# A forward substitution spread over 128 partitions, and two scratch buffers exchanged, in a gated DeltaNet layer

## The chip, the cores and the metric

The kernel runs on one core of a Trainium2 chip. The metric is the device time of one execution in microseconds (us). A core has five engines that each take their own instructions in order: TensorE (PE) for matmuls, VectorE (DVE), ScalarE (ACT), GpSimd (POOL) and SyncE (SP), which here only issues DMA transfers. PE's weight loads are listed apart, as PEld. An engine waits for another by semaphores.

## The reference

One decoder layer over 1024 positions and a model width of 2048, in float32. A combined projection gives q, k, v of eight DeltaNet heads (group A), and u, v, z of eight channel groups with spatial gating (group B). Their outputs are joined and projected by `w_out`. In group A a triangular system is solved for each head and each chunk of 64 positions:

```python
L = jnp.where(strict, jnp.einsum('bhnid,bhnjd->bhnij', kb, k) * decay, 0.0)
rhs = jnp.concatenate([vb, kb * jnp.exp(gc)[..., None]], axis=-1)
sol = lax.linalg.triangular_solve(L + jnp.eye(C, dtype=L.dtype), rhs,
                                  left_side=True, lower=True, unit_diagonal=True)
...
mix = jnp.concatenate([o_a, o_b], axis=-1) @ w_out[l].astype(x.dtype)
h = h + mix
return rms_norm(h, final_norm_w)
```

## The kernel before

**Stages.** The sequence is worked off in two halves of 512 positions. In each half the projection goes tile by tile of 128 columns: first group A (tiles 0 to 31, in four head pairs), then group B (the blocks `vb` of w_vb, then tiles 32 to 47). After both halves comes the output projection (L1002), which takes seven products of sums of quarters of `w_out` and of the mixed outputs in place of eight products.

**Weights.** A tile has four chunks. SP loads a chunk (`wr`, 256 KB, three buffers), ACT rounds it to `wh` (L136), DVE takes the rest `wl` (L137), and PE does 12 matmuls with them (L238, L239, L241): `wh` with `xh`, `wh` with `xl`, `wl` with `xh`, four times. The loop `run` prepares up to four chunks ahead of the one that PE works on. Names carry tile and chunk: `wl_25_1` is the second chunk of tile 25, `acc_24` the sum of tile 24.

**Side tasks.** What follows a tile (convolution, swaps through DRAM, gates, the DeltaNet steps) is written as generators. `tick` counts down and resumes them between matmuls, so that the numbers which they yield set where their instructions stand among those of the projection. The compiler's scheduler then fixes one order for each engine. `task_z` (tiles 24 to 31) scales the finished tile into `pcz` on DVE (L404) and writes its SiLU `z` on ACT (L544).

**The substitution.** `task_pair` runs once for each head pair and half, eight times. The inverses of the diagonal blocks of 32 x 32 are wanted, 32 of them in a pair: the lower triangles come from DRAM (`ld`) into `fs`, one block on each of 32 partitions; 31 steps of a multiply (L566) and a subtract (L568) turn the identity, in the other half of `fs`, into the inverse; it goes to DRAM (`xd`) and comes back (`tn`, L574) with the positions on the partitions, where it is transposed into `tt` and used in matmuls. `W_DMA1` and `W_DMA2` are the ticks that are left for the transfers.

**Behind it.** The chunk outputs `at` (L649) are added to `o` (L650), normalised (L655 to L661), transposed through DRAM (four `swapo`, L430, then `ut`, L433, both issued by POOL), and multiplied by the gate `z` (L672). `at` and the `sp` of group B's spatial gating share the PSUM banks of `gen_bank`; `s` (L746) reads `sp` and frees one.

**Sums of w_out.** `w_sums` makes, in the first half and in the second, eight steps each: four quarters are loaded (`ws`, L831), combined on DVE (L833 to L837) and stored to DRAM (`wc_d`, L840) for the output projection. It starts `W_SUM0` ticks after it is spawned, and then goes on as its buffers come free.

Of the kernel before, what the change touches and what calls it, by code (L numbers as in the profile page):

```python
# [8 lines left out]
F32 = mybir.dt.float32  # L9
# [3 lines left out]
ALU = mybir.AluOpType  # L13
# [4 lines left out]
P = 128  # L18
DM = 2048
SEQ = 1024  # L20
T = 512
NHALF = SEQ // T
KT = DM // P
NT = T // P
# [7 lines left out]
def kernel(ctx, tc, x_tok, x_t, w_in, w_v0, w_vb, w_out, conv_w, norm_w, a_log, dt_bias,  # L32
                       hn_w, sgu_w, sgu_b, wsp_t, b_sp, fn_w, out):
    nc = tc.nc
# [4 lines left out]
    big = pool("big", bufs=4)  # L39
    wk = pool("wk", bufs=2)  # L40
    sm = pool("sm", bufs=2)
    dr = pool("dr", bufs=2, space=DRAM)
# [8 lines left out]
    def bc(ap, shape):  # L51
        return ap.broadcast_to(shape)
# [21 lines left out]
    for c in range(2):  # L74
        r = slice(c * 64, (c + 1) * 64)
# [378 lines left out]
    W_DMA2 = 18  # L454
# [36 lines left out]
    def task_q(hf, h, st, pr, acc):  # L491
# [32 lines left out]
        if hh == 1:  # L524
            spawn(task_pair(hf, h // 2, st, pr))
# [23 lines left out]
    def task_pair(hf, p, st, pr):  # L549
        gt, heads = st["gt"], pr["hd"]  # L550

        ld, xd = pr["ld"], pr["xd"]
        fs = big.tile([32, 2, 32, 32], F32, tag="b8", name=f"fs{hf}_{p}")
        lu, xu = fs[:, 0], fs[:, 1]
        ldv = ld.rearrange("h t (c s j) (z i) -> s z (h t c) j i", c=2, s=2, z=2)
        for s in range(2):
            nc.gpsimd.dma_start(lu[s * 16:(s + 1) * 16], ldv[s, s])
        nc.gpsimd.memset(xu, 0.0)
        nc.gpsimd.memset(xu.rearrange("u i j -> u (i j)")[:, ::33], 1.0)
        tmp = wk.tile([32, 256], F32, tag="fst", bufs=1, name=f"fst{hf}_{p}")  # L560
        yield W_DMA1

        for k in range(31):
            n, m = 31 - k, k + 1
            tv = tmp[:, 0:n * m].rearrange("u (i j) -> u i j", j=m)
            nc.vector.tensor_tensor(tv, bc(lu[:, k, k + 1:].unsqueeze(2), [32, n, m]),  # L566
                                    bc(xu[:, k:k + 1, 0:m], [32, n, m]), op=ALU.mult)
            nc.vector.tensor_tensor(xu[:, k + 1:, 0:m], xu[:, k + 1:, 0:m], tv, op=ALU.subtract)  # L568
            yield 1
        xdv = xd.rearrange("h t (c s j) i -> s (h t c) (j i)", c=2, s=2)  # L570
        for s in range(2):
            nc.sync.dma_start(xdv[s], xu[s * 16:(s + 1) * 16].rearrange("u i j -> u (i j)"))
        tn = wk.tile([P, 2 * NT, 32], F32, tag="tn", bufs=1, name=f"tn{hf}_{p}")
        nc.sync.dma_start(tn, xd.rearrange("h t p i -> p (h t) i"))  # L574
        yield W_DMA2

        for q in range(0, P, 32):
            nc.vector.transpose(tt[q:q + 32, :, q:q + 32], tn[q:q + 32])
# [2 lines left out]
        for c in range(2):  # L581
            a, b = c * 64, c * 64 + 32
# [3 lines left out]
        for c in range(2):  # L586
            b = c * 64 + 32
            nc.scalar.activation(ys[b:b + 32], yp[b:b + 32], AF.Copy, scale=-1.0)
        yield 3
        for c in range(2):  # L590
            a, b = c * 64, c * 64 + 32
# [3 lines left out]
        for c in range(2):  # L595
            a, b = c * 64, c * 64 + 32
# [48 lines left out]
        for h2, hd in enumerate(heads):  # L645
            nm, o = f"{hf}_{p}_{h2}", hd["o"]
# [28 lines left out]
    def new_pair(hf, p):  # L675
        return dict(kq=big.tile([P, 2, 2, T], F32, tag="b8", name=f"kq{hf}_{p}"),
                    ld=dr.tile([2, NT, P, 64], F32, tag="ld", name=f"ld{hf}_{p}"),
                    xd=dr.tile([2, NT, P, 32], F32, tag="xd", name=f"xd{hf}_{p}"),
                    hd=[{}, {}])

    def group_a(hf, xs, st):
# [86 lines left out]
    def group_b(hf, xs, st):  # L768

        env, sb = {}, {}  # L770
        spawn(w_sums([(hf, k) for k in range(HK)]))
        for blk in range(1, 4):
            for k2 in range(KT // 2):
# [46 lines left out]
    def w_quarter(b, cb, k):  # L820

        return w_out[b[1] * 2 + cb, b[0] * HK + k]

    def w_sums(ck):

        yield W_SUM0
        for cb, k in ck:
            q = {}
            for i, b in enumerate(((1, 1), (0, 1), (0, 0), (1, 0))):
                q[b] = wk.tile([P, 1, T], F32, tag=("cv", "bv")[i // 2], bufs=(3, 2)[i // 2], name=f"ws{cb}_{k}_{i}")  # L830
                nc.sync.dma_start(q[b], w_quarter(b, cb, k))  # L831
            yield 5
            nc.vector.tensor_tensor(q[1, 1], q[1, 1], q[0, 1], op=ALU.subtract)  # L833
            nc.vector.tensor_tensor(q[0, 1], q[0, 1], q[0, 0], op=ALU.subtract)
            yield 1
            nc.vector.tensor_tensor(q[0, 0], q[0, 0], q[1, 1], op=ALU.add)
            nc.vector.tensor_tensor(q[1, 0], q[1, 0], q[0, 0], op=ALU.subtract)  # L837
            yield 1
            for i, b in enumerate(((0, 1), (0, 0), (1, 1), (1, 0))):
                nc.sync.dma_start(wc_d[i, cb, k], q[b].rearrange("p o c -> p (o c)"))  # L840
            yield 3
# [238 lines left out]
```

## Time and profile before

| what | value |
|---|---|
| median of 3 runs | 1778.87 us (1775.11 to 1783.17) |
| the profiled execution | 1779.21 us, span 1777.5 us |
| mean granted clock of PE | 0.992 |
| PE busy | 1728.8 us, 97% |
| DVE busy | 1251.7 us, 70% |
| ACT busy | 738.5 us, 42% |
| POOL busy | 263.6 us, 15% |
| moved by DMA | 277.99 MB, mean 156 GB/s |

The span runs from the first to the last instruction; the execution's own time is 1.7 us longer. An engine's busy time says little of what sets the end: what PE waits for has to be read from its waits, and where a clock below 1.0 stands in a window, its matmuls take longer.

### The profile page before, as it was taken

The numbers are of one execution on the slowest core, as the hardware profiler recorded it, in microseconds if no ns is written. First come the engines' busy times: TensorE is split into PE (matmuls) and PEld (weight loads), VectorE is DVE, ScalarE is ACT, GpSimd is POOL, SyncE is SP. The second block draws the span as 40 slices with busy tenths as digits, with TensorE's granted clock in tenths as the row PEclk, the third lists the DMA queues.
The fourth block names the chain that finished last, engine by engine and source line by source line (L and its number), as shares of the span: only waits on it lengthen the run. The fifth ranks groups of instructions, "written<-read, shape, count | busy, mean of one in ns | idle before, by whom it ended". The sixth has DMA issues, their size and how long they took to land.

```text
span 1777.5 us, 27441 instructions
## 1 busy us (share of the span) xinstructions
PE 1728.8 (97%) x9334; PEld 1456.6 (82%) x9334; DVE 1251.7 (70%) x2945; ACT 738.5 (42%) x1678; POOL 263.6 (15%) x314
## 2 busy tenths in 40 slices
PE   9999999999999999998999999999989999999997
PEld 8778788888997788886878878889878888888885
DVE  7798797987747633757979789793863344767765
ACT  7543544445333222646344444532422234433454
POOL 4110131211201200203012112120020000200211
PEclk9999999999999999999999999999999999999998
DMA  7455445364458734426453645444884466766455
GB/s 239 128 134 145 108 124 144 91 169 133 132 172 260 258 108 126 130 69 153 126 134 92 164 106 149 134 116 117 248 277 133 118 188 199 223 191 193 144 190 190
DMA packets 190046, 277.99 MB, mean 156 GB/s; under 512 B 38064, under 2 KB 70864, under 8 KB 189648
## 3 DMA queue, kind: packets, MB, share of 16 engines
q1 hardware_dynamic: 185216, 263.60, 50.9%
q0 software_dynamic: 4544, 12.62, 3.0%
q8 instruction: 73, 1.20, 0.3%
q14 instruction: 69, 0.57, 0.1%
q10 hardware_dynamic: 144, 0.01, 0.0%
HBM read 220.54 MB, written 55.61 MB: 155 GB/s over the span
## 4 chain that ended last, share of the span: by engine, by line
PE 54%; DVE 9%; DMA 7%; ACT 2%; issue 2%; SPq 0%; POOL 0%; DVEq 0%; ACTq 0%; POOLq 0%
PE oa L1002 12%; PE acc L238 10%; PE acc L241 10%; PE acc L239 10%; PE vb L788 7%; DMA ws<-w_out 1%; DVE wl L137 1%; DVE cv L413 1%; DMA xres<-x_tok 1%; DMA wc_d<-ws 1%; DVE c L914 1%; PE p L621 1%; PE sp L744 1%; DMA wr<-w_in 1%; PE at L649 1%
## 5 line engine op out<-in xcount | busy, mean ns | idle before, releaser
L238 PE MATMUL acc<-xh,wh 128*128 128x512 f32 x1472 | 591.8, 402 | 1.0 <-ACT wh L136 1.0
L241 PE MATMUL acc<-xh,wl 128*128 128x512 f32 x1472 | 576.9, 392 | 7.5 <-DVE wl L137 7.5
L239 PE MATMUL acc<-xl,wh 128*128 128x512 f32 x1472 | 575.8, 391 | 0.0
L136 ACT CAST wh<-wr 128x512 fp32r<-128x512 f32 x368 | 225.7, 618 | 427.7 <-PE acc L239 270.6
L137 DVE TENSOR_TENSOR wl<-wr,wh 128x512 fp32r<-128x512 f32 x368 | 258.2, 704 | 154.2 <-ACT wh L136 151.2
L241 PEld LDWEIGHTS acc<-xh,wl 128*128 128x128 f32 x1472 | 277.1, 188 | 67.0 <-DVE wl L137 9.0
L238 PEld LDWEIGHTS acc<-xh,wh 128*128 128x128 f32 x1472 | 278.0, 189 | 57.7 <-issue 3.0
L239 PEld LDWEIGHTS acc<-xl,wh 128*128 128x128 f32 x1472 | 278.0, 189 | 51.5 <-issue 0.2
L1002 PE MATMUL oa<-who,a 128*128 128x512 f32 x864 | 267.9, 390 | 0.2 <-ACT who L136 0.2
L1002 PEld LDWEIGHTS oa<-who,a 128*128 128x128 f32 x864 | 162.6, 188 | 34.7 <-ACT who L136 0.6
L1002 PE MATMUL oa<-wlo,a 128*128 128x512 f32 x432 | 168.7, 390 | 0.6 <-DVE wlo L137 0.5
L137 DVE TENSOR_TENSOR wlo<-wro,who 128x512 fp32r<-128x512 f32 x108 | 79.4, 738 | 52.7 <-ACT who L136 52.2
L413 DVE SCALAR_TENSOR_TENSOR cv<-pc,cw,cv 128x511 f32<-128x511 f32 (+1 forms) x144 | 109.1, 758 | 9.6 <-ACT cv L410 8.2
L788 PE MATMUL vb<-whvb,xh 128*128 128x256 f32 x384 | 110.5, 288 | 0.0
L788 PE MATMUL vb<-wlvb,xh 128*128 128x256 f32 x384 | 108.6, 283 | 0.0
L788 PE MATMUL vb<-whvb,xl 128*128 128x256 f32 x384 | 108.6, 283 | 0.0
L136 ACT CAST who<-wro 128x512 fp32r<-128x512 f32 x108 | 66.6, 618 | 96.6 <-PE oa L1002 63.7
L1002 PEld LDWEIGHTS oa<-wlo,a 128*128 128x128 f32 x432 | 81.3, 188 | 18.5 <-DVE wlo L137 1.7
L566 DVE TENSOR_TENSOR fst<-fs 32x31 f32<-32x31 f32 (+15 forms) x248 | 89.3, 360 | 4.3
L568 DVE TENSOR_TENSOR fs<-fs,fst 32x31 f32<-32x31 f32 (+15 forms) x248 | 89.0, 359 | 4.1
L625 ACT ACTIVATE o<-p,g_egs 64x128 f32<-64x128 f32 x128 | 46.5, 363 | 84.3 <-DVE vz L624 81.6
L952 POOL TENSOR_TENSOR c<-c,fw 128x512 f32<-128x512 f32 x24 | 37.6, 1596 | 254.6 <-ACT sqh L950 254.6
(245 smaller groups left out, 2379.2 us busy)
## 6 DMA issues: line engine op xcount, KB each, us to landing
wr<-w_in SPq DMA_DIRECT2D x368, 256.0 KB, 3.3
ws<-w_out SPq DMA_DIRECT2D x64, 256.0 KB, 4.0
wc_d<-ws SPq DMA_DIRECT2D x64, 256.0 KB, 3.6
wro<-wc_d SPq DMA_DIRECT2D x64, 256.0 KB, 2.8
ar<-mix_d SPq DMA_DIRECT2D x56, 256.0 KB, 3.5
wrvb<-w_vb SPq DMA_DIRECT2D x48, 256.0 KB, 2.7
wro<-w_out SPq DMA_DIRECT2D x48, 256.0 KB, 2.8
xr<-x_t SPq DMA_DIRECT2D x32, 256.0 KB, 4.2
```

Of the source, the lines that this page charges most:

```text
L136: nc.scalar.copy(hi, src)
L137: nc.vector.tensor_tensor(lo, src, hi.bitcast(F32), op=ALU.subtract)
L238: nc.tensor.matmul(acc, hi[:, kk, :], xh, start=(k == 0), stop=False)
L239: nc.tensor.matmul(acc, hi[:, kk, :], xl, start=False, stop=(last and lo is None))
L241: nc.tensor.matmul(acc, lo[:, kk, :], xh, start=False, stop=last)
L413: nc.vector.scalar_tensor_tensor(cv[:, s:], acc[:, :T - s], w, cv[:, s:], op0=ALU.mult, op1=ALU.add)
L566: nc.vector.tensor_tensor(tv, bc(lu[:, k, k + 1:].unsqueeze(2), [32, n, m]), bc(xu[:, k:k + 1, 0:m], [32, n, m]), op=ALU.mult)
L568: nc.vector.tensor_tensor(xu[:, k + 1:, 0:m], xu[:, k + 1:, 0:m], tv, op=ALU.subtract)
L625: nc.scalar.activation(hd["o"][ra, t, :], pp[rq, :], AF.Copy, scale=gt["egs"][rq, h, t:t + 1])
L788: nc.tensor.matmul(a, l[:, tsl], r[:, k % 2, :], start=fl, stop=sp_, skip_group_check=True)
L952: nc.gpsimd.tensor_tensor(c, c, env["fw"][q], op=ALU.mult)
L1002: nc.tensor.matmul(acc[t], l[:, tsl], r[:, 0, :], start=fl, stop=sp_, skip_group_check=True)
```

## The change

The 32 systems of a pair are spread over 128 partitions: partition g*32 + u holds system u and those columns j of the inverse for which j mod 4 = g, eight of them. Step k then touches only the first k//4 + 1 of the eight columns, where before it touched k + 1. `fs` is loaded four times over, so eight loads take the place of two, four issued by POOL and four by SP; POOL's memsets are smaller, and one is made for each quarter of the partitions. The result goes out in one transfer instead of two. It comes back in pieces of 8 elements (32 bytes) into a new tile `tg`, where before a piece was 32 elements (128 bytes), and ACT copies `tg` into `tn` in natural order. `w_sums` takes its quarters from the buffers of `o` (2) and `gae` (3) instead of those of `cv` (3) and `bv` (2).

```diff
@@ task_pair
-        fs = big.tile([32, 2, 32, 32], F32, tag="b8", name=f"fs{hf}_{p}")
-        lu, xu = fs[:, 0], fs[:, 1]
+        fs = big.tile([P, 2, 32, 32], F32, tag="b8", name=f"fs{hf}_{p}")
+        lu, xu = fs[:, 0], fs[:, 1, 0:8].rearrange("u a (b m) -> u (a b) m", m=8)
         ldv = ld.rearrange("h t (c s j) (z i) -> s z (h t c) j i", c=2, s=2, z=2)
-        for s in range(2):
-            nc.gpsimd.dma_start(lu[s * 16:(s + 1) * 16], ldv[s, s])
-        nc.gpsimd.memset(xu, 0.0)
-        nc.gpsimd.memset(xu.rearrange("u i j -> u (i j)")[:, ::33], 1.0)
-        tmp = wk.tile([32, 256], F32, tag="fst", bufs=1, name=f"fst{hf}_{p}")
+        xf = xu.rearrange("u i m -> u (i m)")
+        nc.gpsimd.memset(xf, 0.0)
+        for g in range(4):
+            for s in range(2):
+                (nc.gpsimd, nc.sync)[g % 2].dma_start(lu[g * 32 + s:(g + 1) * 32:2], ldv[s, s])
+            nc.gpsimd.memset(xf[g * 32:(g + 1) * 32, 8 * g:8 * g + 33 * 7 + 1:33], 1.0)
+        tmp = wk.tile([P, 80], F32, tag="fst", bufs=1, name=f"fst{hf}_{p}")
         yield W_DMA1
 
         for k in range(31):
-            n, m = 31 - k, k + 1
+            n, m = 31 - k, k // 4 + 1
             tv = tmp[:, 0:n * m].rearrange("u (i j) -> u i j", j=m)
-            nc.vector.tensor_tensor(tv, bc(lu[:, k, k + 1:].unsqueeze(2), [32, n, m]),
-                                    bc(xu[:, k:k + 1, 0:m], [32, n, m]), op=ALU.mult)
+            nc.vector.tensor_tensor(tv, bc(lu[:, k, k + 1:].unsqueeze(2), [P, n, m]),
+                                    bc(xu[:, k:k + 1, 0:m], [P, n, m]), op=ALU.mult)
             nc.vector.tensor_tensor(xu[:, k + 1:, 0:m], xu[:, k + 1:, 0:m], tv, op=ALU.subtract)
             yield 1
-        xdv = xd.rearrange("h t (c s j) i -> s (h t c) (j i)", c=2, s=2)
-        for s in range(2):
-            nc.sync.dma_start(xdv[s], xu[s * 16:(s + 1) * 16].rearrange("u i j -> u (i j)"))
+        nc.sync.dma_start(xd, xf)
+        tg = wk.tile([P, 4, 2 * NT, 8], F32, tag="tg", bufs=1, name=f"tg{hf}_{p}")
+        nc.sync.dma_start(tg, xd.rearrange("(g u c s) (r m) -> (c s r) (g u) m", g=4, s=2, c=2, m=8))
+        yield W_DMA2 - 2
         tn = wk.tile([P, 2 * NT, 32], F32, tag="tn", bufs=1, name=f"tn{hf}_{p}")
-        nc.sync.dma_start(tn, xd.rearrange("h t p i -> p (h t) i"))
-        yield W_DMA2
+        nc.scalar.copy(tn.rearrange("p u (m g) -> p g u m", g=4), tg)
+        yield 2
@@ w_sums
-                q[b] = wk.tile([P, 1, T], F32, tag=("cv", "bv")[i // 2], bufs=(3, 2)[i // 2], name=f"ws{cb}_{k}_{i}")
+                q[b] = wk.tile([P, 1, T], F32, tag=("o", "gae")[i // 2], bufs=(2, 3)[i // 2], name=f"ws{cb}_{k}_{i}")
```

From here on the changed kernel's lines are four higher (L746 is L750), and inside `task_pair` up to three (L566 is L569, L568 L571).

**Tile 24 to 25, first pair.** On ACT before, at the change from tile 24 to 25 in the first pair of the first half (`cv_17` belongs to tile 17):

```order
L136 CAST wh_24_3_1295<-wr_24_3_1293 128x512
L410 ACTIVATE cv_17_1286<-pc_17_1284,cw 128x512
L136 CAST wh_25_0_1320<-wr_25_0_1318 128x512
L530 ACTIVATE cv_17_1286<-cv_17_1286 128x512
L136 CAST wh_25_1_1352<-wr_25_1_1350 128x512
L136 CAST wh_25_2_1374<-wr_25_2_1372 128x512
L136 CAST wh_25_3_1400<-wr_25_3_1398 128x512
L544 ACTIVATE z_0_1394<-pcz_0_1392 128x512
```

And at the same place with the change:

```order
L136 CAST wh_24_3_1304<-wr_24_3_1302 128x512
L410 ACTIVATE cv_17_1295<-pc_17_1293,cw 128x512
L530 ACTIVATE cv_17_1295<-cv_17_1295 128x512
L544 ACTIVATE z_0_1403<-pcz_0_1401 128x512
L136 CAST wh_25_0_1329<-wr_25_0_1327 128x512
L136 CAST wh_25_1_1361<-wr_25_1_1359 128x512
```

`z_0`, which needs all of tile 24, has moved from behind the four casts of tile 25 to ahead of them. DVE there with the change (the rows left out are 12 more of the substitution):

```order
L425 STREAM_TRANSPOSE pc_17_1293<-cv_17_1295 128x4x4x32
L404 TENSOR_TENSOR pcz_0_1401<-acc_24_1308,rb_715 128x512
L569 TENSOR_TENSOR fst_0_1243<-fs_0_1229 128x31
...
L571 TENSOR_TENSOR fs_0_1229<-fs_0_1229,fst_0_1243 128x25x2
L569 TENSOR_TENSOR fst_0_1243<-fs_0_1229 128x48
L137 TENSOR_TENSOR wl_25_0_1330<-wr_25_0_1327,wh_25_0_1329 128x512
L571 TENSOR_TENSOR fs_0_1229<-fs_0_1229,fst_0_1243 128x24x2
```

`pcz_0` and 15 instructions of the substitution now stand ahead of `wl_25_0`, and 19 more follow before `wl_25_1`; before, `wl_25_0`, the transpose and `wl_25_1` stood ahead of the first step of the substitution, and `pcz_0` behind its 15th. The second half has the same order.

**Ahead of `s_0`, half 1.** On DVE before, the last part of the chain from `at_3_0` to `s_0` (`ws_5_i` are the quarters of the sixth step of the sums):

```order
L137 TENSOR_TENSOR wl_41_1_6312<-wr_41_1_6309,wh_41_1_6311 128x512
L833 TENSOR_TENSOR ws_5_0_6996<-ws_5_0_6996,ws_5_1_6998 128x512
L834 TENSOR_TENSOR ws_5_1_6998<-ws_5_1_6998,ws_5_2_7000 128x512
L836 TENSOR_TENSOR ws_5_2_7000<-ws_5_2_7000,ws_5_0_6996 128x512
L137 TENSOR_TENSOR wl_41_2_6330<-wr_41_2_6327,wh_41_2_6329 128x512
L672 SCALAR_TENSOR_TENSOR o_3_0_5711<-ut_3_0_5703,hnw,z_6_4785 128x512
L837 TENSOR_TENSOR ws_5_3_7002<-ws_5_3_7002,ws_5_2_7000 128x512
L746 SCALAR_TENSOR_TENSOR s_0_6156<-sp_0_6151,lnw,brow 128x512
```

And with the change:

```order
L137 TENSOR_TENSOR wl_41_1_6352<-wr_41_1_6349,wh_41_1_6351 128x512
L676 SCALAR_TENSOR_TENSOR o_3_0_5751<-ut_3_0_5743,hnw,z_6_4824 128x512
L137 TENSOR_TENSOR wl_41_2_6370<-wr_41_2_6367,wh_41_2_6369 128x512
L750 SCALAR_TENSOR_TENSOR s_0_6196<-sp_0_6191,lnw,brow 128x512
```

The sums have left this stretch, and `o` stands ahead of `wl_41_2`.

**Sums among the weight loads.** On SP with the change, a piece of the stage between `wr_35_0` and `wr_38_2`:

```order
L187 DMA wr_36_0_6781<-w_in 128x512
L844 DMA wc_d<-ws_2_1_6693 128x512
L844 DMA wc_d<-ws_2_2_6695 128x512
L844 DMA wc_d<-ws_2_0_6691 128x512
L844 DMA wc_d<-ws_2_3_6697 128x512
L835 DMA ws_3_0_6799<-w_out 128x512
L835 DMA ws_3_2_6803<-w_out 128x512
L835 DMA ws_3_1_6801<-w_out 128x512
L835 DMA ws_3_3_6805<-w_out 128x512
L187 DMA wr_36_1_6807<-w_in 128x512
```

Eight transfers of the sums stand between two chunks of a tile. Before, the loads and stores of the sums were spread from tile 31 through the `vb` blocks up to `wr_42_3`, and in this place stood `wr_35_1` to `wr_45_0` with only loads of x and stores of the mixed outputs between them.

## Rows read from the trace of the kernel before

**Rows 1.** The page's busy table: busy us, share of span, instructions.

```profile
PE 1728.8 (97%) x9334; PEld 1456.6 (82%) x9334; DVE 1251.7 (70%) x2945; ACT 738.5 (42%) x1678; POOL 263.6 (15%) x314
```

**Rows 2.** Waits of PE: total us, times, longest us.

```profile
PE at L649 <- DVE s L746: 10.7, 2, 5.6
...
PE ds L632 <- DVE vz L624: 4.0, 10, 0.9
...
PE wp L611 <- DVE wq L612: 2.8, 3, 1.1
```

**Rows 3.** Windows behind the two long waits: us, busy of engines, PEclk, DMA share, GB/s.

```profile
580.00:584.00 4.00, 3.93 (x14) 3.52 (x15) 2.81 (x5) 0.91 (x5) 1.66 (x1) 0.53 0.77 232
1305.00:1311.00 6.00, 5.42 (x22) 4.97 (x22) 4.42 (x8) 2.43 (x10) 1.96 (x2) 0.52 0.84 281
```

**Rows 4.** The page's costliest groups: busy us, mean ns | idle before.

```profile
L566 DVE TENSOR_TENSOR fst<-fs 32x31 f32<-32x31 f32 (+15 forms) x248 | 89.3, 360 | 4.3
L568 DVE TENSOR_TENSOR fs<-fs,fst 32x31 f32<-32x31 f32 (+15 forms) x248 | 89.0, 359 | 4.1
```

**Rows 5.** Timeline of DVE, first pair: start, duration, instruction.

```profile
114.42 0.17 DVE L566 TENSOR_TENSOR fst<-fs 32x31 f32<-32x31 f32 x1
...
115.98 0.21 DVE L568 TENSOR_TENSOR fs<-fs,fst 32x60 f32<-32x60 f32 x1
116.23 0.24 DVE L566 TENSOR_TENSOR fst<-fs 32x87 f32<-32x87 f32 x1
...
120.19 0.67 DVE L404 TENSOR_TENSOR pcz<-acc,rb 128x512 f32<-128x512 f32 x1
```

**Rows 6.** Timeline of ACT at the same place.

```profile
116.42 0.62 ACT L136 CAST wh<-wr 128x512 fp32r<-128x512 f32 x1 [1.64 <-DMA wr<-w_in]
120.89 0.63 ACT L544 ACTIVATE z<-pcz 128x512 f32<-128x512 f32 x1 [3.85 <-DVE pcz L404]
```

**Rows 7.** Timeline of PE, last and first matmuls of tiles 24 and 25.

```profile
844.05 0.39 PE L241 MATMUL acc<-xh,wl 128*128 128x512 f32 x1
844.27 0.39 PE L238 MATMUL acc<-xh,wh 128*128 128x512 f32 x1
```

**Rows 8.** DMA issues of the page: count, KB each, median us to landing.

```profile
ws<-w_out SPq DMA_DIRECT2D x64, 256.0 KB, 4.0
wc_d<-ws SPq DMA_DIRECT2D x64, 256.0 KB, 3.6
...
ut<-swapo POOLq DMA_DIRECT2D x16, 256.0 KB, 3.9
...
fs<-ld POOLq DMA_DIRECT2D x16, 64.0 KB, 4.2
...
tn<-xd SPq DMA_DIRECT2D x8, 128.0 KB, 4.7
```

**Rows 9.** Timeline of POOL, pair 3 of half 1.

```profile
562.69 2.98 POOL L430 DMA_DIRECT2D swapo<-ut  x4 [1.47 <-DVE ut L425]
572.30 0.57 POOL L433 DMA_DIRECT2D ut<-swapo  x1 [6.64 <-DMA swapo<-ut]
```

**Rows 10.** Timeline of POOL, the same steps for an earlier pair.

```profile
468.98 0.77 POOL L430 DMA_DIRECT2D swapo<-ut  x1 [4.54 <-DVE ut L425]
...
476.05 0.56 POOL L433 DMA_DIRECT2D ut<-swapo  x1 [2.94 <-PE vb L788]
```

**Rows 11.** Timeline of DVE, end of pair 3's chain in half 1.

```profile
577.91 0.75 DVE L672 SCALAR_TENSOR_TENSOR o<-ut,hnw,z 128x512 f32<-128x512 f32 x1 [1.59 <-DMA ut<-swapo]
578.58 0.69 DVE L837 TENSOR_TENSOR ws<-ws,ws 128x512 f32<-128x512 f32 x1
```

**Rows 12.** Window of the sums of w_out in half 1; columns as in rows 3.

```profile
514.00:604.00 90.00, 83.20 (x468) 71.59 (x467) 66.24 (x160) 31.83 (x81) 13.38 (x15) 0.96 0.80 258
```

**Rows 13.** DMA around the landing of tn, 155.5 to 157.2.

```profile
DMA packets 1164, 0.45 MB, mean 264 GB/s; under 512 B 1005, under 2 KB 1005, under 8 KB 1164
...
q1 hardware_dynamic: 1164, 0.45, 105.5%
```

More of the change, by code (lines that the diff above doesn't have):

```diff
@@ L677, in new_pair @@
                     ld=dr.tile([2, NT, P, 64], F32, tag="ld", name=f"ld{hf}_{p}"),
-                    xd=dr.tile([2, NT, P, 32], F32, tag="xd", name=f"xd{hf}_{p}"),
+                    xd=dr.tile([P, 256], F32, tag="xd", name=f"xd{hf}_{p}"),
                     hd=[{}, {}])
```

## Prediction

> **What bounds the kernel now.** I read the busy table first: TensorE (PE) works 97% of the span [rows 1]. So only what makes PE wait, or slows its clock, counts, and VectorE (DVE) time saved is worth nothing where PE does not wait for it. The waits of PE come next [rows 2]: the largest group is L649 waiting for `s` (L746), 10.7 us in two waits, one in each half, the longest 5.6 (so 5.6 and 5.1). Ten waits at L632 give 4.0, three at L611 2.8. Third, the clock after the two long waits: the granted clock averages 0.53 in 580 to 584 and 0.52 in 1305 to 1311 [rows 3], that is mostly the lower of its two levels. PE lost about 3.9 x 0.47 = 1.9 us there in half 1 and 5.4 x 0.48 = 2.6 in half 2. Together the two places cost 10.7 + 4.5 = 15.2 us. No other stage around the change makes PE wait over 1.1 us at a time.
>
> **The substitution itself.** Its 496 instructions cost DVE 89.3 + 89.0 = 178 us, 22.3 a pair [rows 4]. They work on 31 to 256 elements a partition, the new ones on 8 to 76, and one with 60 elements took 0.21 us [rows 5]. 62 x 0.21 = 13 us a pair: DVE gets some 74 us back over eight pairs. PE's own waits behind DVE inside those stretches are the small ones of L632 and L611, 6.8 us in all [rows 2]. I take 3 us of them as gained (bounds 0 and 6.8). The memset on POOL is shorter, the new ScalarE (ACT) copy is of the size class of a cast, 0.62 us at most [rows 6], eight times, on an engine that is idle more than half of the span: nothing, unless its input is late (below).
>
> **Tile 24 to 25 in pair 0 (a loss, both halves).** The new order has `pcz_0`, which needs the finished tile 24, ahead of everything that tile 25 needs. ACT's row shows `z_0` now ahead of `CAST wh_25_0`; before, it stood behind all four casts of tile 25. DVE's row shows 15 substitution instructions between `pcz_0` and `wl_25_0`, and 19 more ahead of `wl_25_1`; before, two of tile 25's chunks were split before the substitution began. Engines take their rows in order, so PE must wait. Call T the end of tile 24. `pcz_0` 0.67 [rows 5], `z_0` 0.63, the cast 0.62 [rows 6], 0.2 for the hand-overs: PE starts tile 25 at T + 2.1. It does two matmuls of 0.227 us [rows 7], then the third needs `wl_25_0`. On DVE, 15 instructions start 0.25 us apart (116.23 after 115.98, with 60 elements, [rows 5]): 0.8 + 15 x 0.25 + 0.7 = T + 5.25, and with the hand-over PE goes on at T + 5.35, having done 0.45 of work: 4.9 lost. `wl_25_1` ends 19 x 0.25 + 0.7 = 5.45 us later, while PE has 10 + 2 matmuls, 2.72 us: 2.7 lost. That is 7.6 a half. The clock: waits of about 2 us do not occur in this trace; waits of about 1 us were followed by no fall, waits of 5 by one that cost 1.9 to 2.6. I take 1.3 between them: 8.9 a half, **+18 us**. Bounds: at 0.17 us an instruction, the shortest row of [rows 5], the three waits are 2.1, 1.6 and 1.2, with no fall 2 x 4.9 = +10; with the fall of half 2 behind them 2 x (7.6 + 2.6) = +20. The loads of `fs` cannot hide it: the fourth one on POOL comes behind two memsets that wait for earlier loads, so two landings of 4.2 us [rows 8] stand in a row before the first substitution. That comes out near T + 0.8 by the times at which `ld` lands before; later, it adds to the loss.
>
> **The waits at L649 (a gain, both halves).** The chain that ends them runs from `at_3_0` through o, its rsqrt, POOL, four `swapo` transfers and one load of `ut`, to o (L672) and `s` (L746). In the row of before, sums of w_out (`ws_4`, `ws_5`) stand between these steps on DVE, each waiting for its own load; in the row of the change none does. From the first `swapo` issue to the load of `ut` it took 572.30 - 562.69 = 9.6 us [rows 9], against 476.05 - 468.98 = 7.1 where no w_out traffic ran [rows 10]: 2.5 less. The load then took until 577.91, 5.6 us [rows 11], against a median of 3.9 [rows 8]: 1.7 less. L837 leaves the stretch between o and `s` (0.69, [rows 11]) and another sum that between POOL and the transpose, about 0.5. Sum 5.4; PE reaches L649 four matmuls earlier, which takes 0.9 back. Of 5.6 us about 1.1 stays, and by the short waits no fall of the clock. Half 2 likewise. Gain 10.7 - 2.2 + 4.5 = **-13 us** (bounds 0, if `swapo` and `ut` are late for another reason, and -15).
>
> **The sums of w_out (a loss).** Before, 64 transfers of 256 KB a half run in a stretch of 90 us, 514 to 604 in half 1, at 258 GB/s with DMA 0.80 busy [rows 12]. Tied to the buffers of o and gae, they start only when pair 3 lets go of them: in SP's row nearly all of them stand between `wr_35_0` and `wr_38_2`. That is 27 chunks of 12 x 0.227 = 2.72 us, 74 us of PE work, with about 60 + 27 + 4 transfers, 23.8 MB: 320 GB/s would be needed to keep up. At 258 it takes 92 us. The buffers give the same: a step needs a store to land (3.6), a load (4.0) [rows 8], three dependent sums of 0.69 [rows 11] and some issue time, 10 to 12 us, and eight steps 80 to 96. So 6 to 22 us are missing, and the SP queue passes this on to the weight loads. Against it stand the chunks that are loaded ahead, three or four, 8 to 11 us. I take 3 us a half, **+6** (bounds 0 and 2 x 12 = +24). The Trainium skill ("DMA: Bandwidth & Descriptors", section Specifications) puts the HBM limit per core near 358 GB/s; by that rule the stage would fit and this term be 0. The trace does not show that rate: its stage reached 258, with waits for buffers in it.
>
> **The gather (`tg`).** It moves the 128 KB of `tn` in 4096 pieces of 32 bytes instead of 1024 of 128. In 1.7 us around its landing 1164 packets, 1005 of them small, filled the engines' time (105.5%) [rows 13]. At that rate 4096 take 6.9 us, 5.2 more, and 4.7 [rows 8] becomes 9.9 to landing. The order puts it one chunk behind the weight load whose cast follows the copy on ACT. With four chunks ahead (10.9 us) less that chunk, the copy and the cast (0.4 and 0.62), 7.2 us are left: hidden at 4.7, late by 2.7 at 9.9. That is 0 to 22 us over eight pairs; I take **+3**, since the wait at tile 25 lets loads run ahead first. The skill's same page and section ask for 512 bytes or more per transfer for full rate; by that rule both gathers are slow ones, which the small packets' full share bears out, and it gives no figure for 32 against 128.
>
> **Sum.** The profiled execution took 1779.2 us, 0.3 above the median of 1778.9. 1779.2 - 3 + 18 - 13 + 6 + 3 = **1790 us**. A difference under 0.5% (8.9 us) can hardly be told from none here; 1790 lies 2 above that bound.
>
> **Rivals.**
> 1. *The sums bind.* If transfers stay at 250 to 260 GB/s and only 8 us are absorbed, the sums cost +22, not +6: 1806. For it: the missing 6 to 22 us. Against it: DVE is free of pair 3 in that stage. It shows as waits on `wl` or `wh` in tiles 35 to 46. 17%.
> 2. *Both hidden costs are nothing.* Sums and gather fit: 1790 - 9 = 1781, no measurable change. For it: the chunks loaded up to 11 us ahead. By the rule of the Trainium skill on the HBM limit (above) the sums would fit; no row shows such a rate. 26%.
> 3. *Tile 25 costs its least, and it gets faster.* The substitution's instructions are so short now that each costs the 0.17 us of the shortest row: PE waits 4.9 us a half, in pieces too short for the clock to fall. With the gain at L649 whole (15), the small waits gone whole (6.8), sums and gather hidden: 1779.2 + 10 - 15 - 6.8 = 1767. For it: the fixed cost is most of a short instruction's time. Against it: the next one starts 0.25 us later, not 0.17. It decides at 6.3 us a half: below that the other terms at their best bring over 0.5%. 13%.
> 4. *L649 waits on.* If `swapo` and `ut` are as slow as before, the gain is 0 to 4: about 1800. 5%.
>
> **Chances and range.** The forecast, 1784 to 1797, has 39%; about 24 of it lie above 1787.8. Slower by over 0.5%: 24 + 17 + 5 = 46%. Within: 15 + 26 = 41%. Faster: 13%. The range 1768 to 1806 reaches to the centres of both outer rivals.
>
> **What would show it.** PE waits of about 2, 2.7 and 2.7 us at the first chunks of tile 25, released by ACT `wh` and DVE `wl`, near 116 and 850. L649 waits of about 1 us and a clock of 1.0 behind them. L566's successor at 0.20 us. In 600 to 690 DMA at 0.8 or more and some waits on `wl`. Wrong would be a tile 25 without waits, waits at L649 as long as before, or ACT's copy holding back casts in all pairs.

## Result and profile after

The changed kernel takes 1822.61 us (median; 1822.39 to 1823.13) against 1776.99 for the kernel before on the same chip: ratio 1.0251, 95% interval 1.023 to 1.0271. It is slower by 45 us, outside the predicted range of 1768 to 1806. The profiled span is 1820.7 us (before 1777.5), at a mean granted clock of 0.984 (0.992).

DVE did get faster, and PE did not profit: the substitution's two lines fell from 178.3 us of DVE to 119.0 (62.2 + 56.8), 59 us against the 74 of the forecast. The busy line of the page, against [rows 1]:

```profile
PE 1742.8 (96%) x9334; PEld 1465.3 (80%) x9334; DVE 1214.9 (67%) x2945; ACT 739.8 (41%) x1686; POOL 273.0 (15%) x354
```

The waits of PE (line, who it waits for, us in total, times, longest), against [rows 2]:

```profile
PE acc L241 <- DVE wl L137: 21.8, 12, 5.5
PE yp L597 <- ACT ys L592: 16.7, 6, 4.2
PE p L625 <- DVE state L637: 9.7, 9, 1.2
PE acc L238 <- ACT wh L136: 4.9, 3, 2.0
...
PE ds L636 <- DVE vz L628: 2.1, 8, 0.3
PE wp L615 <- DVE wq L616: 2.0, 3, 0.7
...
PE at L653 <- DVE s L750: 0.7, 2, 0.4
```

And two lines of the kernel before that [rows 2] does not have:

```profile
PE yp L593 <- ACT ys L588: 1.2, 2, 0.8
...
PE p L621 <- DVE state L633: 0.9, 4, 0.2
```

`at` on `s`, 10.7 us before, is gone as forecast. New are the waits of `yp` on ACT's `ys` (`ys` is minus `yp`, made in between two sets of matmuls), of `p` on `state`, and more of L241 on `wl` (7.5 us before). The windows of the clock (us, PE busy with count, PEld, DVE, ACT, POOL, granted clock, DMA share, GB/s) show what the longer waits leave behind, stretches at 0.50, the lower of the clock's two levels; the one from 580 is where the clock of [rows 3] had fallen, the one from 600 is the stage that the sums moved to:

```profile
118.70:125.50 6.80, 4.61 (x11) 3.65 (x12) 5.97 (x27) 1.14 (x2) 0.00 (x0) 0.50 0.27 80
299.60:306.40 6.80, 5.22 (x40) 4.40 (x41) 4.92 (x21) 3.54 (x10) 0.61 (x1) 0.50 0.39 102
...
1053.90:1060.70 6.80, 6.80 (x44) 5.67 (x45) 4.93 (x21) 2.00 (x5) 0.61 (x1) 0.50 0.45 119
...
580.00:590.00 10.00, 10.00 (x46) 8.27 (x45) 4.00 (x9) 2.50 (x4) 4.42 (x6) 1.00 0.49 123
...
600.00:690.00 90.00, 88.81 (x408) 73.76 (x407) 50.55 (x87) 21.55 (x36) 11.21 (x12) 1.00 0.77 250
```

Tile 25 waits as forecast: PE's timeline (start, length; in brackets the idle time before and who ended it), then DVE's with the substitution standing ahead of `wl_25_0`:

```profile
117.01 0.50 PE L238 MATMUL acc<-xh,wh 128*128 128x512 f32 x1 [1.95 <-ACT wh L136]
...
120.89 0.80 PE L241 MATMUL acc<-xh,wl 128*128 128x512 f32 x1 [3.15 <-DVE wl L137]
```

```profile
115.09 0.69 DVE L404 TENSOR_TENSOR pcz<-acc,rb 128x512 f32<-128x512 f32 x1 [3.58 <-PE acc L241]
...
120.03 0.21 DVE L569 TENSOR_TENSOR fst<-fs 128x48 f32<-128x48 f32 x1
120.15 0.68 DVE L137 TENSOR_TENSOR wl<-wr,wh 128x512 fp32r<-128x512 f32 x1
```

The part that the prediction did not see is in pairs 1 and 2 of both halves. ACT's timeline around pair 1 of half 1, first where the copy stands, then where `ys` stands, 40 us later:

```profile
263.04 0.65 ACT L578 COPY tn<-tg 128x256 f32<-128x256 f32 x1 [5.93 <-DMA tg<-xd]
263.49 0.62 ACT L136 CAST wh<-wr 128x512 fp32r<-128x512 f32 x1
...
265.61 0.63 ACT L465 ACTIVATE kq<-cv 128x512 f32<-128x512 f32 x1 [0.97 <-DVE cv L413]
...
286.84 0.31 ACT L441 ACTIVATE sqq<-pc 128x128 f32<-128x128 f32 x1 [1.52 <-DMA pc<-swapq]
...
288.83 0.61 ACT L465 ACTIVATE kq<-cv 128x512 f32<-128x512 f32 x1
...
298.56 0.31 ACT L441 ACTIVATE sqk<-pc 128x128 f32<-128x128 f32 x1 [4.50 <-DMA pc<-swapk]
...
299.74 0.60 ACT L136 CAST wh<-wr 128x512 fp32r<-128x512 f32 x1
300.36 0.76 ACT L592 ACTIVATE ys<-yp 32x256 f32<-32x256 f32 x2
```

And the same place of the kernel before (pair 1, half 1):

```profile
278.14 0.63 ACT L465 ACTIVATE kq<-cv 128x512 f32<-128x512 f32 x1 [0.70 <-DVE cv L413]
...
287.82 0.31 ACT L441 ACTIVATE sqk<-pc 128x128 f32<-128x128 f32 x1 [0.66 <-DMA pc<-swapk]
...
288.25 0.76 ACT L588 ACTIVATE ys<-yp 32x256 f32<-32x256 f32 x2
```

Three things are to be seen. The copy waits 5.93 us for the gather with a cast and `kq` of the convolution behind it. `kq` of a later tile stood behind the four squares of q (`sqq`) here before too, but two casts stood ahead of the squares, which then waited for nothing; now the squares come first and wait 1.52 us for a swap, with `kq` behind them. And three squares of k (`sqk`) and a cast stand ahead of `ys`, where one square stood: from the first `sqk` to `ys` it is 1.8 us, where it was 0.4. From the start of this tile's `pc` (L404) on DVE to the start of the second half of `ys` on ACT, the timeline gives 14.7 to 17.0 us in the six places of the kernel before (pairs 0 to 2 of both halves) and 16.9 to 19.0 with the change. PE had 15.5 to 16.9 us of other work for that stretch; with the change it has 13.3 to 15.7 in four of the six places, since `pc` also starts later. A chain that just fitted no longer does.

### The profile page after: what moved, and what is told of

Same layout as the page of the kernel before. It is cut to its first block, busy times and chain, and to the rows that moved or that the text cites. A ratio compares the mean times of both kernels' runs of the same rounds, so it can differ in the third digit from the quotient of the medians.

```text
span 1820.7 us, 27563 instructions
## 1 busy us (share of the span) xinstructions
PE 1742.8 (96%) x9334; PEld 1465.3 (80%) x9334; DVE 1214.9 (67%) x2945; ACT 739.8 (41%) x1686; POOL 273.0 (15%) x354
## 4 chain that ended last, share of the span: by engine, by line
PE 61%; DVE 15%; DMA 12%; ACT 5%; issue 5%; SPq 1%; POOL 0%; DVEq 0%; ACTq 0%; POOLq 0%
PE oa L1006 14%; PE acc L241 10%; PE acc L238 10%; PE acc L239 10%; PE vb L792 5%; DMA wr<-w_in 3%; DVE wl L137 3%; DMA pc<-swapk 2%; DVE cv L413 2%; DVE fst L569 2%; DVE fs L571 2%; PE ds L636 1%; PE p L625 1%; DMA tg<-xd 1%; ACT wh L136 1%
## 5 line engine op out<-in xcount | busy, mean ns | idle before, releaser
L241 PE MATMUL acc<-xh,wl 128*128 128x512 f32 x1472 | 583.5, 396 | 21.8 <-DVE wl L137 21.8
L239 PE MATMUL acc<-xl,wh 128*128 128x512 f32 x1472 | 582.0, 395 | 0.0
L137 DVE TENSOR_TENSOR wl<-wr,wh 128x512 fp32r<-128x512 f32 x368 | 265.2, 725 | 142.5 <-ACT wh L136 139.6
L241 PEld LDWEIGHTS acc<-xh,wl 128*128 128x128 f32 x1472 | 280.5, 191 | 85.6 <-DVE wl L137 27.2
L637 DVE SCALAR_TENSOR_TENSOR state<-state,gam,ds 128x128 f32<-128x128 f32 x128 | 44.0, 344 | 51.6 <-PE ds L636 50.3
L792 PEld LDWEIGHTS vb<-whvb,xh 128*128 128x128 f32 x384 | 73.7, 192 | 2.1 <-ACT vn L798 2.0
```

Source lines behind the costliest of these rows:

```text
L137: nc.vector.tensor_tensor(lo, src, hi.bitcast(F32), op=ALU.subtract)
L239: nc.tensor.matmul(acc, hi[:, kk, :], xl, start=False, stop=(last and lo is None))
L241: nc.tensor.matmul(acc, lo[:, kk, :], xh, start=False, stop=last)
L637: nc.vector.scalar_tensor_tensor(S, S, gt["gam"][:, c, 2 * p + h2, t:t + 1], ds, op0=ALU.mult, op1=ALU.add)
L792: nc.tensor.matmul(a, l[:, tsl], r[:, k % 2, :], start=fl, stop=sp_, skip_group_check=True)
```

## Experiments

All ratios are to the kernel before on the same chip, with 95% intervals.

**The parts alone.** `e1_sums_only` is the kernel before with one line changed:

```diff
-tag=("cv", "bv")[i // 2], bufs=(3, 2)[i // 2]
+tag=("o", "gae")[i // 2], bufs=(2, 3)[i // 2]
```

> The kernel before with only the buffers of the sums of w_out changed. If the two parts act apart: the two L649 waits and the slow clock behind them go (14 us), tiles 35 to 46 get waits of some 8 us on wl, so about 1771 us, 6 under before. If the L649 gain needs the shorter substitution: those waits stay and only the loss comes, about 1785.

1775.34 us, ratio 0.9983 (0.9967 to 1.0), nearer to the first expectation than to the rival's. Its waits of PE:

```profile
PE acc L241 <- DVE wl L137: 13.4, 9, 3.2
...
PE at L649 <- DVE s L746: 1.6, 2, 0.8
```

The wait on `s` goes by this line alone, and most of it is given back as waits on `wl`. `e2_subst_only` is the rest of the change, without that line.

> The changed kernel with the sums of w_out in their old buffers. If the parts act apart: after's 1822.6, plus the 14 us of L649 back, less the 8 of the sums, about 1828 us, with tile 25, yp and p waits as in after. If much of the loss comes from the sums' new place: under 1815.

1825.6 us, ratio 1.0275 (1.0253 to 1.0297): the substitution's edit carries the whole loss. `ys` 12.2 us, `p` on `state` 11.2, `at` on `s` 9.5.

**The copy.** `e3_copy_pool` moves it to GpSimd, `e4_no_copy` leaves it out:

```diff
-        nc.scalar.copy(tn.rearrange("p u (m g) -> p g u m", g=4), tg)
+        nc.gpsimd.tensor_copy(tn.rearrange("p u (m g) -> p g u m", g=4), tg)
# e4 instead
+        tn = tg.rearrange("p g u m -> p u m g")
```

> The changed kernel with the copy of tg into tn on GpSimd instead of ScalarE. Theory ACT queue (the copy holds ScalarE for the whole landing of the gather, and casts, kq and the squares ahead of ys with it): the yp waits (16.7 us) and the slow clock behind them (about 11) go, about 1796 us; tile 25 and p waits stay. Rival gather (the 32-byte gather itself comes too late, whoever copies): yp still waits 10 us or more, 1812 to 1825.

> The changed kernel without the copy: the transposes and the matmuls read tg through a strided view. Theory ACT queue: like the copy on GpSimd, about 1796 us, ScalarE waits for no gather. Rival gather: VectorE's transposes wait for the landing with the weight splits behind them, yp or wl waits of 10 us or more, 1812 to 1825.

1816.1 us (1.0211; 1.0188 to 1.0234) and 1818.28 us (1.0216; 1.0185 to 1.0247). Both miss the theory of the copy on ACT's queue. ACT no longer waits for the gather, but DVE's transposes do: `tt`, which waits 22.9 us for the copy in the changed kernel, still waits 14.5 us for GpSimd's copy in the one and 19.8 for `tg` itself in the other.

**The gather apart from the order.** `e5_b_gather` gives the kernel before the gather in 32-byte pieces and the copy; `e6_plain_gather` gives the changed kernel a read of whole rows:

```diff
# e5, in the kernel before
-        nc.sync.dma_start(tn, xd.rearrange("h t p i -> p (h t) i"))
+        nc.sync.dma_start(tg, xd.rearrange("h t p (g m) -> p g (h t) m", g=4))
+        nc.scalar.copy(tn.rearrange("p u (g m) -> p g u m", g=4), tg)
# e6, in the changed kernel
-        nc.sync.dma_start(tg, xd.rearrange("(g u c s) (r m) -> (c s r) (g u) m", g=4, s=2, c=2, m=8))
+        nc.sync.dma_start(tg, xd.rearrange("p (g u m) -> p g u m", g=4, u=2 * NT))
```

> The kernel before, with its own substitution and its two loads of L on GpSimd, but with tg gathered in 32-byte pieces and copied into tn by ScalarE; its order around the copy is that of the kernel before (the copy stands inside tile 5 for pair 1, not ahead of tile 13's first cast). Theory of the order (instructions that wait for transfers stand ahead of ready work in the changed kernel): 1777 to 1784 us, waits of PE on ys under 4 us in all and tile 25 without waits. Rival, the 32-byte gather and the copy themselves: 1795 or more, with the waits on ys as in the changed kernel (over 12 us) and ACT waiting for tg.

> The changed kernel, but tg is read from xd in whole rows of 1 KB, not in 32-byte pieces; the values in tn are then in the wrong places, all instructions and their order are the same. Theory of the order: 1812 to 1823 us, because what stands ahead stays ahead; the copy still waits, by some 2 us less a pair. Rival, the 32-byte pieces: 1790 to 1800, with the waits on ys back to some 1 to 3 us.

e5: 1777.05 us, 0.9985 (0.9969 to 1.0). The gather and the copy cost nothing there, although SyncE's next issue took 3.2 to 5.9 us behind the gather. In e5 the copy of pair 1 stands behind tile 5's casts and waits 1.17 us:

```profile
265.27 1.13 ACT L136 CAST wh<-wr 128x512 fp32r<-128x512 f32 x2
267.57 0.41 ACT L577 COPY tn<-tg 128x256 f32<-128x256 f32 x1 [1.17 <-DMA tg<-xd]
```

e6: 1807.61 us, 1.0161 (1.0145 to 1.0177), 15 us under the changed kernel and between the two expectations: with the changed order the pieces matter after all. The order of e6 is that of the changed kernel but for three of DVE's 2945 rows; the values in `tn` are in the wrong places. The read lands in 3.6 us instead of 5.4 (medians of the DMA issues), and PE waits 5.4 us for `ys` instead of 16.7. How a landing of 2 us less gets there can be followed in pair 1: e6's copy, `kq` and the `pc` of a later tile, then the changed kernel's `pc` (its copy and `kq` are shown above):

```profile
260.99 0.67 ACT L578 COPY tn<-tg 128x256 f32<-128x256 f32 x1 [4.06 <-DMA tg<-xd]
...
263.58 0.63 ACT L465 ACTIVATE kq<-cv 128x512 f32<-128x512 f32 x1 [0.97 <-DVE cv L413]
...
280.61 0.68 DVE L404 TENSOR_TENSOR pc<-acc,rb 128x512 f32<-128x512 f32 x1
```

```profile
283.87 0.68 DVE L404 TENSOR_TENSOR pc<-acc,rb 128x512 f32<-128x512 f32 x1
```

Copy and `kq` come 2.0 us sooner, the `pc` that starts the chain to `ys` 3.3 us. In the six places of e6 that chain still takes 16.4 to 18.3 us, so the pieces hardly lengthen it; but it starts sooner, and PE has 15.7 to 19.9 us of work to cover it. A second reason stands on SyncE's queue. The changed kernel, then e6 (start, length of the issue):

```profile
257.45 0.38 SPq L575 DMA_DIRECT2D tg<-xd  x1
257.92 3.92 SPq L187 DMA_DIRECT2D wr<-w_in  x1
```

```profile
257.27 0.33 SPq L575 DMA_DIRECT2D tg<-xd  x1
257.69 0.38 SPq L187 DMA_DIRECT2D wr<-w_in  x1
```

The issue behind the 4096 pieces takes 2.5 to 4.1 us in all eight pairs.

**The order.** `e7_ld_pool` and `e8_one_step_later` change the engines' order with one edit each:

```diff
# e7
-                (nc.gpsimd, nc.sync)[g % 2].dma_start(lu[g * 32 + s:(g + 1) * 32:2], ldv[s, s])
+                nc.gpsimd.dma_start(lu[g * 32 + s:(g + 1) * 32:2], ldv[s, s])
# e8
-    W_DMA2 = 18
+    W_DMA2 = 19
```

> The changed kernel, with all eight loads of L on GpSimd's queue and none on SyncE's. The arithmetic, the gather, the copy and the sums are the same; but in the order pcz_0 and z_0 again stand behind tile 25's chunks, ds_0_0_7 ahead of p_0_0_1_7, and pair 1's copy stands in tile 5, some 14 rows of ScalarE later. Theory of the order: 1772 to 1785 us, tile 25 without waits of over 1 us, waits on ys under 6 us in all. Rival, gather and copy: only tile 25's 15 us go, 1805 to 1810.

> The changed kernel with one more step between the gather's issue and the use of tn (19 instead of 18): yp moves from tile 18's first chunk to its second, and ds_0_0_7 stands ahead of p_0_0_1_7 again; the copy still stands ahead of tile 13's first cast, and tile 25 keeps its order. Theory of the order: the waits of p on the state (some 10 us with their clock) go, those on ys and at tile 25 stay: 1808 to 1816 us. Rival: if the order of p and ds is only a sign of a late VectorE, p still waits and the time stays at 1820.

e7: 1797.91 us, 1.0109 (1.0094 to 1.0124), 25 us less than the changed kernel, but 18 to 19 more than the kernel before. Its waits of PE:

```profile
PE yp L597 <- ACT ys L592: 15.5, 5, 4.4
...
PE vb L792 <- ACT vn L798: 8.4, 2, 5.0
...
PE p L625 <- DVE state L637: 0.7, 3, 0.2
```

Tile 25's waits and those of `p` are gone, those on `ys` stay. It misses the theory by 13 us, and the rival too. A part of what is left is new, the 8.4 us of `vb`. In this order the copy of pair 3 stands ahead of `vn` (L798), which takes the finished sums of a block `vb` out of PSUM. ACT in half 2:

```profile
1223.22 0.65 ACT L578 COPY tn<-tg 128x256 f32<-128x256 f32 x1 [7.78 <-DMA tg<-xd]
...
1224.72 1.18 ACT L798 COPY vn<-vb 128x256 f32<-128x256 f32 x4
```

With the two falls of the clock there (4.6 us lost) this is 13 us of waiting for the gather, at a place where the changed kernel waits 1.5 us and the kernel before not at all. e8: 1812.89 us, 1.0192 (1.0174 to 1.021), as forecast in size but not by the way: `p` still waits 8.5 us in nine waits, because the order put other pairs of `p` and `ds` out of turn (`p_0_1_0_7` ahead of `ds_0_1_1_6`) in place of the one that it mended.

**An earlier start of the substitution.** `e9_memsets_first` puts the four small memsets ahead of the loads of L; `e10_first_and_pool` adds e7's edit.

```diff
+            nc.gpsimd.memset(xf[g * 32:(g + 1) * 32, 8 * g:8 * g + 33 * 7 + 1:33], 1.0)
+        for g in range(4):
             for s in range(2):
                 (nc.gpsimd, nc.sync)[g % 2].dma_start(lu[g * 32 + s:(g + 1) * 32:2], ldv[s, s])
-            nc.gpsimd.memset(xf[g * 32:(g + 1) * 32, 8 * g:8 * g + 33 * 7 + 1:33], 1.0)
```

> The changed kernel, with the four small memsets of the diagonal ahead of the eight loads of L instead of between them, so that no load on GpSimd waits behind a memset that waits for a load; the order of the other engines is that of the changed kernel. Theory: the copy, the transposes and the load of ut stand ahead of ready work and cost what their transfers are late. The loads go out some 4 us earlier, so the substitution starts about 13.5 us behind the store of gl instead of 19.4, ScalarE waits for tg 1 us or less instead of 6 a pair, the waits on ys (16.7) fall to under 6; tile 25 and p on the state stay: 1795 to 1808 us. Rival: the substitution ends when its tiles' turn comes, not when the loads land; then the time stays at 1815 to 1823.

> Both moves: the small memsets ahead of the loads of L, and all eight loads on GpSimd's queue. The order is that of the run with the loads on GpSimd (tile 25's chunks ahead of pcz_0, the copy of pair 1 inside tile 5, ds ahead of p), but the loads no longer wait in a row for one another, so the substitution starts some 14 to 17 us behind the store of gl instead of 33, and tg lands ahead of its copy. Theory (order plus late transfers): no waits on ys above 2 us, 1765 to 1778 us, faster than the kernel before. Rival: copy, gather and the shared queue cost by themselves: 1790 or more.

1821.93 us (1.0237; 1.0217 to 1.0257) and 1801.74 us (1.0126; 1.0107 to 1.0146): both rivals were right. In e9 the last load of pair 1 is issued 3.9 us sooner behind the store of `gl`, but the first step starts 18.5 us behind it against 19.3, some 9 us after the last load landed: it starts when DVE's order comes to it, not when the loads land.

**ys behind the squares.** `e11_ys_on_vector` makes `ys` on VectorE, `e12_pool_and_ys` adds e7's edit:

```diff
-            nc.scalar.activation(ys[b:b + 32], yp[b:b + 32], AF.Copy, scale=-1.0)
+            nc.vector.tensor_scalar(ys[b:b + 32], yp[b:b + 32], -1.0, None, op0=ALU.mult)
```

> The changed kernel, with ys (minus yp) made by VectorE instead of ScalarE; nothing else is edited. In ScalarE's order of the changed kernel three squares of k (sqk), which wait for the load of swapk, stand ahead of ys in pairs 1 and 2 of both halves; in that of the kernel before one does. On VectorE, ys stands behind the convolution of the same tile and no transfer. Theory (ys behind the squares): the waits of PE on ys (16.7 us) fall under 4 us, most of the half-clock spells behind them go, tile 25 and p on the state stay: 1796 to 1806 us. Rival: the lateness only moves on, to the cast of the next tile's first chunk, which also stands behind those squares: 1812 or more, with waits on wh or wl of tiles 19, 21 and 23 in their place.

> Both edits: all loads of L on GpSimd's queue, which takes the order at tile 25 and of p and ds back, and ys on VectorE. Theory: 1772 to 1784 us, about the kernel before or a little faster; waits on ys under 4 us, none over 1.5 at tile 25. Rival (the lateness moves on): 1790 to 1798, as with the loads on GpSimd alone.

1815.69 us (1.0213; 1.0192 to 1.0234) and 1790.93 us (1.0076; 1.0053 to 1.0099). The wait on `ys` is gone, but 10.0 and 8.7 us come back as waits of `up` (L610) on `tt` (L601). The lateness moves on, to another place than the rival named. DVE in e11:

```profile
296.91 0.86 DVE L592 TENSOR_SCALAR ys<-yp 32x256 f32<-32x256 f32 x2
302.47 0.17 DVE L477 TENSOR_SCALAR ssk<-ssk 128x4 f32<-128x4 f32 x1 [4.70 <-ACT sqk L441]
...
306.16 0.41 DVE L601 COPY tt<-yp 32x256 f32<-32x256 f32 x1
```

`ssk` waits for the late squares, with `wl` and `tt` behind it. Reordering `ys` alone does not help, since the squares themselves are late.

**No wait for the gather.** `e13_early_tg` gathers `tg` from L's rows at the pair's start, so that nothing waits for it; `e14_early_tg_pool` adds e7's edit. `e15_early_whole_rows` and `e16_early_rows_pool` are the same two with whole rows in place of 32-byte pieces. None of the four uses the inverse, so `tn` holds other values.

```diff
-        nc.sync.dma_start(tg, xd.rearrange("(g u c s) (r m) -> (c s r) (g u) m", g=4, s=2, c=2, m=8))
# at the pair's start, e13 and e14; then e15 and e16
+        nc.sync.dma_start(tg, ld[0].rearrange("t p i -> (t p i)").rearrange("(u p g m) -> p g u m", u=2 * NT, p=P, g=4))
+        nc.sync.dma_start(tg, ld[0].rearrange("t p i -> (t p i)").rearrange("(p g u m) -> p g u m", u=2 * NT, p=P, g=4))
```

> The changed kernel, but tg is gathered, in the same 32-byte pieces, from the rows of L that the pair has just stored, at the pair's start, and no longer from xd behind the substitution; the inverse is then not used, so tn holds other values. No instruction waits for the gather any more. In the order, tile 25 and p/ds are as in the changed kernel, and one square of k instead of three stands ahead of ys. Theory (half of the loss is the wait for tg ahead of the convolution's chain): no waits of the copy and of tt, waits on ys under 4 us, 1793 to 1802 us. Rival: the swap transfers are late for another reason (more and smaller transfers, the loads of L): waits on ys of 8 us or more, 1810 or more.

> The same early gather, and all eight loads of L on GpSimd's queue, which takes the order at tile 25 and of p and ds back to that of the kernel before. Theory: the two causes add up; without both the changed kernel is as fast as the kernel before or faster: 1764 to 1778 us, with the gain at L653 (waits of 1 us) and the sums' waits on wl left. Rival: some 10 to 15 us stay open: 1785 or more.

1818.01 us (1.0211; 1.0179 to 1.0243) and 1795.98 us (1.0091; 1.0066 to 1.0115), with 15.0 and 20.9 us on `ys`: missed. But the gather had only moved its hold on SyncE's queue, to just ahead of the load of `swapk` that the squares wait for. SyncE in e13:

```profile
292.64 0.64 SPq L565 DMA_DIRECT2D tg<-ld  x1
293.37 3.37 SPq L187 DMA_DIRECT2D wr<-w_in  x1
296.90 0.33 SPq L433 DMA_DIRECT2D pc<-swapk  x1
```

> As the run with the early gather, but tg is read in whole rows of 1 KB, which does not hold SyncE's queue (in 32-byte pieces the next issue behind the gather takes 3 to 4 us instead of 0.4, and in that run it stood ahead of the load of swapk that the squares wait for). The inverse is not used. Order of tile 25 and of p/ds as in the changed kernel, two squares of k ahead of ys. Theory (the gather's wait in ScalarE's queue and its hold on SyncE's make the chain conv, swap, squares, ys late): waits on ys 6 us or less, 1796 to 1806 us. Rival: the chain is late by ScalarE's order alone (kq behind the squares of q, squares of k ahead of ys): waits on ys 10 us or more, 1810 or more.

> The same, and all eight loads of L on GpSimd's queue, which takes the order of tile 25 and of p/ds back. Theory: 1774 to 1786 us, waits on ys 6 us or less. Rival (ScalarE's order alone): 1790 or more.

1806.13 us (1.0158; 1.0141 to 1.0174), at the upper edge of the theory, with 5.8 us on `ys`, and 1781.34 us (1.0008; 0.9993 to 1.0022). From e13 to e15 only the pieces change and the order hardly does, and no instruction waits for the landing in either: the hold on SyncE's queue is worth 12 us by itself there. With neither the gather's wait and hold nor the order that the split loads bring, the changed kernel is as fast as the kernel before. PE in e16:

```profile
PE acc L241 <- DVE wl L137: 14.5, 7, 5.9
PE yp L597 <- ACT ys L592: 10.6, 5, 3.4
...
PE at L653 <- DVE s L750: 1.1, 2, 0.7
```

The 10.6 us on `ys` that are left are more than the 6 expected, and three falls of the clock behind them cost 6.8 more; against them stands the gain at L653. `vb` waits 1.0 us here, not the 8.4 of e7.

**The gather on GpSimd.** `e17_gather_on_pool` issues the gather from GpSimd; `e18_pool_gather_ys` has e17's, e7's and e11's edits.

> The changed kernel with the gather of tg, in its 32-byte pieces, on GpSimd's queue instead of SyncE's. In ScalarE's order the copy then stands behind kq of tile 12's head and behind the next cast, no longer ahead of them. Theory: no hold on SyncE's queue and the chain no longer behind the copy: waits on ys 8 us or less, 1803 to 1813 us; tile 25 and p/ds stay. Rival: GpSimd needs longer to issue 4096 pieces than SyncE, and tn is late: 1820 or more.

> Three edits that leave the arithmetic as it is: the loads of L and the gather on GpSimd's queue, ys on VectorE. Theory: tile 25, p/ds, the hold on SyncE and ys behind the squares are gone, 1772 to 1784 us, level with the kernel before; left are the sums' waits and some of up on tt. Rival: GpSimd's one queue now delays L and tg: 1791 or more, with waits of wp and vb behind a late tt.

1825.88 us (1.0285; 1.025 to 1.032) and 1808.41 us (1.0168; 1.0151 to 1.0184): the first no better than the changed kernel, the second worse than e12, as the rivals had it. GpSimd needs 1.71 us for the issue, behind its other transfers, and the gather then lands in 6.0 us (5.4 from SyncE):

```profile
264.33 1.71 POOL L575 DMA_DIRECT2D tg<-xd  x1
```

No version tried beats the kernel before by more than the measurement can tell.

## Why the prediction was wrong

**Two causes, and they add.** Four kernels make a table (medians in us):

| | loads of L on two queues | all on GpSimd |
|---|---|---|
| gather behind the substitution | 1822.6 (1.0251) | 1797.9 (1.0109, e7) |
| early, in whole rows | 1806.1 (1.0158, e15) | 1781.3 (1.0008, e16) |

Down the columns it is 16.5 and 16.6 us, along the rows 24.7 and 24.8 (by the ratios 17 and 18, 25 and 27): 41 to 43 of the 45 us lost, with next to no overlap. That the totals add so closely is in part luck, for the places differ: with the loads on two queues the gather costs waits on `ys`, with the loads on GpSimd some of that and 13 us ahead of `vn` (e7).

**L649** (forecast -13): right. 10.7 - 0.7 = 10.0 us of waits and the two falls of the clock (4.5) are gone, -14.5; e1 shows that the sums' buffers do it.

**Tile 25** (+18): right in place and mechanism. Waits 1.95 + 3.15 + 0.31 in half 1 and 1.95 + 2.37 + 0.69 in half 2, 10.4 us (forecast 15.2); the clock fell during the second wait in both halves, over 4.61 and 4.82 us of PE work at 0.50, 4.7 us lost (forecast 2.6). Together 15.1. The split of the loads over two queues brings that order, e7 takes it back.

**Sums** (+6): right in place, near in size. Five waits on `wl`, at 678, 690, 701, 1443 and 1453 us, 1.19 + 1.78 + 2.75 + 1.08 + 1.67 = 8.5; the stage ran at 250 GB/s, near the 258 of [rows 12]. The rate by the Trainium skill's HBM limit ("DMA: Bandwidth & Descriptors", section Specifications) was not reached over the stage here either. The prediction's words that no row shows such a rate hold for the stage alone: from 1308 to 1310 us the trace of before has 355 GB/s.

**Small waits** (-3): right; L632 and L611 fell from 6.8 to 2.1 + 2.0 us, 2.7 gained. What the sum had at nothing, without a reason, is `p` on `state`, which rose from 0.9 to 9.7, +8.8. In pairs 0 to 2 of both halves PE's order has `ds_0_0_0_7` and `p_0_0_1_7` (half, pair, head, step) exchanged, so that PE stands at `p` for `state` with `ds` of the other head behind it: six waits of 1.21 to 1.25 us, and three of 0.73 to 0.88 beside them in half 2. I compared the order at the two places that I priced, and not along the recurrence. e7, with the order as before, has 0.7 us there.

**The gather** (+3, bounds 0 to 22): this is the step that failed, with what hangs on it. I measured its cover in weight chunks: "four chunks ahead (10.9 us)" before PE runs dry behind the copy. The chunks did hold; what stood behind the copy and could not wait was `kq`, and behind it the chain of convolution, swaps through DRAM, squares and `ys`, with 15.5 to 16.9 us of PE work over 14.7 to 17.0 us of chain. The cost: 16.7 - 1.2 = 15.5 us of waits on `ys`, and five falls of the clock behind them, over 5.22 + 3.40 + 3.40 + 6.80 + 6.45 us of PE work at half clock, 12.6 lost. That is 28.1 us, above the upper bound. e6 splits it: with whole rows in the same order 5.4 us of waits and 5.1 lost to the clock are left there, so some 19 us go with the 32-byte pieces, and some 9 stay with the changed order, in which the chain is still some 2 us longer than before. The whole kernel gains 15 us in e6 and 16.5 in e15, as other waits grow. The landing itself was mis-sized the other way, 5.4 us where the argument from packets gave up to 9.9: the small term rested on two errors of opposite sign.

The sum by these readings: -14.5 + 15.1 + 8.5 - 2.7 + 8.8 + 28.1 = +43.3, against 1820.7 - 1777.5 = 43.2 of span. Forecast was +11.

**The rivals.** None held. L649 did not wait on, the waits on `wl` that the first rival named came but cost 8.5 us and not 22, the hidden costs were not nothing, and tile 25 did not cost its least. The prediction named "ACT's copy holding back casts in all pairs" as what would make it wrong; that was near, but e3 and e4 show that the copy is not it: whoever takes `tg` first waits.

**Open.** Why the scheduler orders tile 25 and `p`/`ds` as it does when the loads are split is argued from the orders, not shown. Which rows of the order make the chain to `ys` longer is not isolated by a run: in pair 1 of half 1, 1.4 of the 1.6 us by which it grew lie between the first `sqk` and `ys`, but e11 took `ys` from there and the lateness went on to `tt`. How e6's gain divides between the sooner landing and the freer queue is not shown for the gather behind the substitution.

## What to carry to other kernels

Where each engine's order is fixed ahead, a small edit (here, which queue issues eight loads, e7) changes the order of unrelated work, and a transfer that the old order covered is waited for in the new one: follow not only the instruction that waits, but the longest chain that stands behind it, up to the place where PE needs its end. The same gather and copy cost nothing in one order (e5) and some 15 us in another (e6). A wait that is taken off one engine or one instruction (e3, e4, e11) comes back nearby; it went only where the transfer landed sooner (e6) or well ahead of its use (e15, e16).

## What the runs showed of the hardware

- Behind the gather of 4096 pieces of 32 bytes SyncE's next issue took 2.5 to 4.1 us in eight of eight pairs of the changed kernel, and 0.38 behind whole rows (e6, median). Issued from GpSimd the gather's own issue took 1.71 us (e17).
- It landed in 5.4 us (median), the 1024 pieces of 128 bytes of before in 4.7 [rows 8], whole rows in 3.6 (e6).
- The changed kernel has seven waits of PE of 2 to 4 us; at six of them lies a stretch of 3.4 or 6.8 us at a granted clock of 0.50, and at the one of 2.75 us (from 701 us on) none. The kernel before has one, which the prediction left aside: 3.38 us up to 1741, and 2.9 us of PE work at 0.50 behind it.
